# Modulation vectors on TensorE: groups of two row blocks in place of one

## The chip, the cores and the metric

One core of one Trainium2 chip. The metric is the device time of one execution in microseconds; the median of three runs of the kernel before is 2575.46 us (2573.92 to 2581.18).

## What is computed

A backbone of two layers over 256 latent and 256 context tokens, 1024 channels wide. Each layer makes six modulation vectors per stream from a conditioning vector, and uses them around its norms and residuals:

```python
mod  = jnp.split((sc @ p['w_mod'] + p['b_mod'])[:, None, :], 6, axis=-1)
modc = jnp.split(sc_ctx @ p['w_mod'] + p['b_mod'], 6, axis=-1)
h = modulate(rmsnorm(x, p['norm1_g']), mod[0], mod[1])
y, yc = token_mixer(h, hc, p, lambda_init, ctx_out)      # projection, 3 mixers, merge
x = x + mod[2] * y
h2 = modulate(rmsnorm(x, p['norm2_g']), mod[3], mod[4])
x = x + mod[5] * ec_moe(h2, p)                           # 16 experts, top-32 tokens each
```

The context stream goes through the same steps in the first layer. w_mod is 1024 x 6144 per layer, so one vector needs a 1024 x 1024 piece of it: eight row blocks of 128 rows, 512 KB each.

## The kernel before

Everything is computed with the channels on the partitions. A layer is a mixer (`run_blocks`: a list of projection blocks of 128 output channels, 24 matmuls each in three fp32r passes) and then a mixture of experts (`moe`, `body`), whose expert weights stream in through the SP queue. The first layer's mixer runs from about 60 to 930 us, its out-projection to about 990, its experts to about 1480; then the same for the second layer.

The order of all instructions is written out when the kernel is built. The blocks of `run_blocks` are the foreground. Between their matmuls `Background.pump` lets generator tasks (attention heads "diff", long convolutions "hy", the convolution's filters, modulation vectors) run one step each, up to the next `yield wait(...)`. A step may run when the planner's own clock has passed its due time, when a PSUM bank is free, and when its gate, if it has one, is open. The list of live tasks is walked in order, and at most four (WIDTH, first layer) are live in the first place. `until` and `drain` run steps early where the foreground would wait.

Modulation vectors of the first layer come three ways. Vectors 0 and 1 are made in `setup`. Vectors 2, 3 and 4 of layer 0 and 0 and 1 of layer 1 are the task "modN" (line 2020), vector 5 of layer 0 is the task "modA" (line 1584), both by `mod_run` (line 708). `mod_run` keeps `depth` row blocks in flight. For each block it issues four matmuls, one for each 256 of the 1024 columns, into four 32-column tiles of the array (the stationary operand `sc` is 32 columns wide); then it waits for a free "a4" buffer (the gate `room(a4=1)`), issues the next 512 KB load (`mod_load`), and waits for the oldest block in flight and a pause in the planner's time: 6000 ns for modN, 1300 ns for modA. After eight blocks `mod_out` copies the sum out, transposes it on PE and adds the bias; `mod_post` prepares the router (`router_prep`) after vector 4.

The a4 pool has 13 buffers of 512 KB. The projection's raw weights (`wraw`, loaded by `load_block` up to three blocks ahead), their two fp32r halves (`wh`, `wl`), key tiles of the attention and the modulation row blocks (`wm`) share it. `load_block` takes one only while more than one (SPARE) is free. At the start of the first layer's experts, expert weights use it too: `body` fills them, forces the rest of modA (`drain("modA")`, line 1945) and fills on. modN has to be done before the out-projection's `pre_out` (line 1562).

Of the kernel before, what the change touches and what calls it, by code (L numbers as in the profile page):

```python
# [21 lines left out]
KT = 8  # L22
# [249 lines left out]
def wait(*aps, delay=0.0, bank=1, gate=None):  # L272
    return aps, delay, bank, gate
# [135 lines left out]
class Kernel:  # L409
# [298 lines left out]
    def mod_run(self, vs, depth, pause, delay=3000.0):  # L708
        todo = [(l, v, k) for l, v in vs for k in range(KT)]
        raw = deque(self.mod_load(*todo.pop(0)) for _ in range(depth))  # L710
        yield wait(raw[0], delay=delay)
        for l, v in vs:
            acc = self.bank([128, 256], "m")
            for k in range(KT):
                w = raw.popleft()
                for c in range(4):
                    self.mm(acc[c * 32:(c + 1) * 32, :], self.sc[:, k, :], w[:, c * 256:(c + 1) * 256], k == 0, k == KT - 1, 4)
                w = None
                if todo:
                    yield wait(gate=self.room(a4=1))  # L720
                if todo:
                    raw.append(self.mod_load(*todo.pop(0)))
                yield wait(*list(raw)[:1], delay=pause)
            yield wait(acc, bank=0)
            yield from self.mod_out(l, v, acc)
            yield from self.mod_post(l, v)
# [668 lines left out]
    def mixer(self, l):  # L1395
        nc, A = self.nc, self.A
        full = l < L - 1
# [12 lines left out]
        def add(srcs, hl, n, evac, pre=None, drains=()):  # L1410
            bl.append(Block(srcs, hl, n, evac, pre, drains))

        def cols(w, c0, n=128):
            return [((slice(0, 128), slice(0, KT), slice(0, n)), w.rearrange("(k p) n -> p k n", p=128)[:, :, c0:c0 + n])]
# [161 lines left out]
        for j in range(KT):  # L1576
            def ev_o(p, j=j):
                for s in range(ns):
                    sl = slice(s * 256, s * 256 + 256)
                    self.stt(self.xT[:, j, sl], p[:, sl], self.modc[l][:, 2, j, s:s + 1], self.xT[:, j, sl], OP.mult, OP.add)  # L1580
                self.bg.add("post", lambda task, j=j: self.post(l, j, nq))
                if j == 4 and full:
                    vs = [(l, 5)]
                    self.bg.add("modA", lambda task: self.mod_run(vs, 2, 1300.0, 19000.0 if full else 11000.0))
            add(cols(A["w_out"][l], j * 128), lambda: self.mg, nt, ev_o, pre_out if j == 0 else None)
        return bl

# [429 lines left out]
    def run(self):  # L2017
        bl = self.mixer(0)
        self.setup(bl)
        self.bg.add("modN", lambda task: self.mod_run([(0, 2), (0, 3), (0, 4), (1, 0), (1, 1)], 1, 6000.0))  # L2020
        for l in range(L):
            if l:
                self.new_arena(3)
                self.lend(2)
                self.bg.add("filter", lambda task: self.transform(task), 2)
            fill, body = self.moe(l)
            self.fill = fill
            self.bg.layer = l
            self.run_blocks(bl)
            body()  # L2030
            if l < L - 1:
                bl = self.next
                for b in bl[EARLY:3]:
                    self.split_block(b)
                self.make_h(self.norm_next(), l + 1)
        self.final()
# [27 lines left out]
```

## Time and profile before

| | us |
|---|---|
| median of three runs | 2575.46 |
| lowest, highest | 2573.92, 2581.18 |
| the profiled execution | 2579.04 |
| its span, first to last instruction | 2577.3 |
| PE busy | 2240.2 |
| DVE busy | 1347.2 |
| ACT busy | 882.1 |
| POOL busy | 794.8 |

The mean granted TensorE clock of the profiled execution is 0.945 of full. PE is the engine of the matrix products, PEld its weight loads, DVE, ACT and POOL the vector, scalar and general engines, SP the queue that issues nearly all DMAs. The profile gives two records to each fp32 matmul. "Idle before" and "waited for" are worked out from semaphore events; a wait is put down to the event that came last.

### The profile page before, as it was taken

What the parts mean: (1) busy time and instruction counts of PE and PEld (TensorE: products, weight loads), DVE (VectorE), ACT (ScalarE), POOL (GpSimd) and SP (SyncE); (2) the same over time, 40 slices, a digit from 0 to 9 for tenths busy, and PEclk for the clock granted to TensorE, in tenths of its full rate; (3) what the DMA queues carried; (4) which work ended last, traced back from release to release, by engine and by line L of the source; (5) the groups of instructions that cost most, each with busy time, mean ns of one, the idle gap of its engine ahead of it and who ended that gap; (6) DMA issues with size and microseconds to landing.
All of it is one profiled execution on the core that took longest, in us unless ns stands there. A gap on an engine that the chain in (4) does not pass through costs nothing.

```text
span 2577.3 us, 38619 instructions
## 1 busy us (share of the span) xinstructions
PE 2240.2 (87%) x14970; PEld 1542.7 (60%) x14970; DVE 1347.2 (52%) x2907; ACT 882.1 (34%) x1933; POOL 794.8 (31%) x775
## 2 busy tenths in 40 slices
PE   6999998989999998989998899899888987656565
PEld 4777776767768775333333378878787864323223
DVE  4778778888672324223333178887887541101011
ACT  4445444555552332101111055556435441000001
POOL 2653433642334541000111055665544430000000
PEclk8999999999999999999999999999989989878787
DMA  9434233221213368899999963333665589999997
GB/s 304 123 122 126 89 109 106 58 66 50 66 58 91 95 252 316 331 428 417 398 400 399 398 185 97 104 95 84 177 190 164 130 317 423 422 424 423 424 423 278
DMA packets 327135, 590.32 MB, mean 229 GB/s; under 512 B 46076, under 2 KB 278184, under 8 KB 299304
## 3 DMA queue, kind: packets, MB, share of 16 engines
q1 hardware_dynamic: 326952, 587.85, 62.2%
q8 instruction: 119, 1.95, 0.3%
q14 instruction: 64, 0.52, 0.1%
HBM read 584.66 MB, written 3.15 MB: 228 GB/s over the span
## 4 chain that ended last, share of the span: by engine, by line
PE 47%; DMA 20%; DVE 20%; issue 4%; ACT 4%; POOL 3%; SPq 1%; DVEq 0%; POOLq 0%; ACTq 0%
PE p L458 44%; DMA mw<-in_moe_w_dram 19%; DVE arena L261 6%; DVE t L261 5%; PE p L469 3%; DVE wl L261 2%; DVE qp L261 2%; ACT arena L261 1%; DMA wm<-in_w_mod_dram 1%; POOL wl L261 1%; SPq L261 1%; POOL arena L261 1%; DVE ma L261 1%; DVE yc L261 1%; ACT wh L261 1%
## 5 line engine op out<-in xcount | busy, mean ns | idle before, releaser
L458 PE MATMUL p<-mw,xg 128*32 128x256 f32 (+1 forms) x3072 | 411.0, 508 | 115.3 <-DMA mw<-in_moe_w_dram 114.4
L458 PE MATMUL p<-hhi,wh 128*128 128x512 f32 (+1 forms) x1344 | 471.4, 363 | 10.1 <-DVE arena L261 7.7
L458 PE MATMUL p<-hlo,wh 128*128 128x512 f32 (+1 forms) x1344 | 458.9, 354 | 1.6 <-POOL hlo L261 0.8
L261 POOL TENSOR_TENSOR wl<-wraw,wh 128x512 fp32r<-128x512 f32 x232 | 342.5, 1478 | 374.8 <-ACT wh L261 251.8
L458 PEld LDWEIGHTS p<-mw,xg 128*32 128x32 f32 (+1 forms) x3072 | 133.7, 129 | 317.1 <-issue 200.0
L458 PE MATMUL p<-hhi,wl 128*128 128x512 f32 (+1 forms) x1344 | 312.9, 361 | 4.5 <-DVE wl L261 4.4
L458 PEld LDWEIGHTS p<-hhi,wh 128*128 128x128 f32 x1344 | 259.4, 193 | 48.5 <-issue 13.3
L458 PEld LDWEIGHTS p<-hlo,wh 128*128 128x128 f32 x1344 | 259.6, 193 | 31.4 <-POOL hlo L261 1.7
L458 PE MATMUL p<-mw,aT 128*32 128x256 f32 (+3 forms) x1760 | 200.4, 475 | 62.5 <-DMA mw<-in_moe_w_dram 58.2
L261 DVE TENSOR_TENSOR wl<-wraw,wh 128x512 fp32r<-128x512 f32 x231 | 217.0, 940 | 57.4 <-ACT wh L261 47.0
L261 ACT ACTIVATE wh<-wraw 128x1024 fp32r<-128x1024 f32 x232 | 241.4, 1053 | 9.0 <-DMA wraw<-in_w_in_dram 6.8
L458 PEld LDWEIGHTS p<-hhi,wl 128*128 128x128 f32 x1344 | 222.0, 194 | 37.0 <-DVE wl L261 5.2
L261 ACT ACTIVATE arena<-p 128x512 f32<-128x512 f32 (+1 forms) x212 | 106.4, 507 | 354.5 <-PE p L458 296.7
L458 PEld LDWEIGHTS p<-mw,aT 128*32 128x32 f32 (+1 forms) x1760 | 79.5, 134 | 172.3 <-issue 109.0
L261 DVE COPY yS<-p 32x512 f32<-32x512 f32 (+1 forms) x60 | 33.4, 556 | 272.9 <-ACT yS L261 272.9
L261 POOL TENSOR_TENSOR sq<-sq,sq 128x512 f32<-128x512 f32 (+1 forms) x6 | 6.3, 1055 | 505.6 <-ACT sq L261 498.8
L458 PE MATMUL p<-yb,wh 128*128 128x512 f32 (+1 forms) x768 | 153.6, 343 | 7.5 <-POOL yb L261 6.8
L261 ACT ACTIVATE arena<-p,t 128x512 f32<-128x512 f32 (+1 forms) x192 | 116.5, 613 | 84.7 <-DVE t L261 82.5
L458 PEld LDWEIGHTS p<-yb,wh 128*128 128x128 f32 x768 | 118.5, 190 | 26.8 <-POOL yb L261 11.6
L261 ACT ACTIVATE s<-p 128x512 f32<-128x512 f32 (+1 forms) x32 | 15.7, 491 | 337.1 <-PE p L458 336.9
L261 ACT ACTIVATE yS<-p 32x256 f32<-32x256 f32 (+2 forms) x84 | 35.3, 420 | 266.2 <-PE p L458 247.1
L469 PE MATMUL p<-cst,arena 128*128 128x128 f32 x608 | 101.0, 290 | 28.8 <-DVE arena L261 27.8
(243 smaller groups left out, 3451.4 us busy)
## 6 DMA issues: line engine op xcount, KB each, us to landing
mw<-in_moe_w_dram SPq DMA_DIRECT2D x171, 2048.0 KB
wraw<-in_w_in_dram SPq DMA_DIRECT2D x152, 512.0 KB
wm<-in_w_mod_dram SPq DMA_DIRECT2D x72, 512.0 KB
mw<-in_moe_w_dram SPq DMA_DIRECT2D x46, 512.0 KB
mw<-in_moe_w_dram SPq DMA_DIRECT2D x17, 1024.0 KB
wraw<-in_w_branch_dram SPq DMA_DIRECT2D x32, 512.0 KB
wm<-in_w_mod_dram SPq DMA_DIRECT2D x5, 2048.0 KB
wraw<-in_w_in_dram SPq DMA_DIRECT2D x32, 256.0 KB
```

Source lines behind the costliest of these rows:

```text
L261: return f(*args, **kw)
L458: self.nc.tensor.matmul(out, lhsT=lhsT, rhs=rhs, start=start, stop=stop, skip_group_check=tiles > 1)
L469: self.nc.tensor.transpose(out, in_, self.ident[:n, :n])
```

## The change

`mod_run` works on `depth` row blocks at a time: the matmuls of all of them, then a gate for `depth` a4 buffers, then `depth` loads, each still 512 KB, then a wait for all of them. modN goes from depth 1 with a pause of 6000 to depth 2 with 12000; modA keeps depth 2, and its pause goes from 1300 to 2600. The start delay of modA loses a branch that was never taken, since the task is only added where `full` holds.

```diff
     def mod_run(self, vs, depth, pause, delay=3000.0):
         todo = [(l, v, k) for l, v in vs for k in range(KT)]
         raw = deque(self.mod_load(*todo.pop(0)) for _ in range(depth))
-        yield wait(raw[0], delay=delay)
+        yield wait(*raw, delay=delay)
         for l, v in vs:
             acc = self.bank([128, 256], "m")
-            for k in range(KT):
-                w = raw.popleft()
-                for c in range(4):
-                    self.mm(acc[c * 32:(c + 1) * 32, :], self.sc[:, k, :], w[:, c * 256:(c + 1) * 256], k == 0, k == KT - 1, 4)
+            for k0 in range(0, KT, depth):
+                for k in range(k0, k0 + depth):
+                    w = raw.popleft()
+                    for c in range(4):
+                        self.mm(acc[c * 32:(c + 1) * 32, :], self.sc[:, k, :], w[:, c * 256:(c + 1) * 256], k == 0, k == KT - 1, 4)
                 w = None
                 if todo:
-                    yield wait(gate=self.room(a4=1))
-                if todo:
+                    yield wait(gate=self.room(a4=depth))
+                for _ in range(min(depth, len(todo))):
                     raw.append(self.mod_load(*todo.pop(0)))
-                yield wait(*list(raw)[:1], delay=pause)
+                yield wait(*raw, delay=pause)
...
-                    self.bg.add("modA", lambda task: self.mod_run(vs, 2, 1300.0, 19000.0 if full else 11000.0))
+                    self.bg.add("modA", lambda task: self.mod_run(vs, 2, 2600.0, 19000.0))
...
-        self.bg.add("modN", lambda task: self.mod_run([(0, 2), (0, 3), (0, 4), (1, 0), (1, 1)], 1, 6000.0))
+        self.bg.add("modN", lambda task: self.mod_run([(0, 2), (0, 3), (0, 4), (1, 0), (1, 1)], 2, 12000.0))
```

## Rows read from the trace of the kernel before

**Rows 1.** The page's table of engines: busy us, share of the span, instructions.

```profile
PE 2240.2 (87%) x14970; PEld 1542.7 (60%) x14970; DVE 1347.2 (52%) x2907; ACT 882.1 (34%) x1933; POOL 794.8 (31%) x775
```

**Rows 2.** Busy us and instructions by stage, granted clock (share of full), DMA share, GB/s.

```profile
60.00:460.00 400.00, 374.88 (x2110) 288.35 (x2109) 313.00 (x657) 184.15 (x396) 193.48 (x210) 0.98 0.37 113
460.00:930.00 470.00, 450.23 (x2409) 356.14 (x2408) 286.33 (x649) 218.41 (x486) 189.45 (x173) 1.00 0.27 76
1000.00:1480.00 480.00, 442.06 (x2273) 176.52 (x2273) 143.99 (x338) 63.70 (x146) 36.77 (x65) 0.99 0.96 391
```

**Rows 3.** Chain that ended last, by line: first of 60 to 460 us, then 1000 to 1480.

```profile
by line: PE p L458 43.8%; DVE arena L261 17.0%; issue 6.7%; DVE t L261 6.0%; PE p L469 3.8%; DVE qp L261 3.2%; ACT arena L261 2.7%; DVE wl L261 1.9%; DVE yc L261 1.8%; POOL arena L261 1.8%; ACT qp L261 1.3%; DVE yd L261 1.0%; DMA wraw<-in_w
by line: PE p L458 64.4%; DMA mw<-in_moe_w_dram 26.3%; PE p L469 2.3%; DVE yS L261 1.3%; ACT yS L261 1.2%; DVE arena L261 1.1%; issue 0.8%; POOL hx L261 0.6%; DVE xg L261 0.5%; DVE s L261 0.4%; DVE sr L261 0.3%; ACT hx L261 0.3%; POOL K L26
```

**Rows 4.** PE's timeline around one modulation group: start us, us, engine, line, operation, out<-in.

```profile
108.42 0.40 PE L458 MATMUL p<-hhi,wh 128*128 128x512 f32 x1
108.66 0.40 PE L458 MATMUL p<-hlo,wh 128*128 128x512 f32 x1
108.98 0.64 PE L458 MATMUL p<-wm,sc 128*32 128x256 f32 x8
109.56 0.50 PE L458 MATMUL p<-hhi,wh 128*128 128x512 f32 x1
109.89 0.40 PE L458 MATMUL p<-hlo,wh 128*128 128x512 f32 x1
```

**Rows 5.** PE's timeline at the end of layer 0's out-projection, modulation groups and top-k transposes.

```profile
985.77 0.64 PE L458 MATMUL p<-wm,sc 128*32 128x256 f32 x8
...
989.04 2.37 PE L458 MATMUL p<-wm,sc 128*32 128x256 f32 x40
...
994.25 0.64 PE L458 MATMUL p<-wm,sc 128*32 128x256 f32 x8
998.54 0.42 PE L469 MATMUL p<-cst,mk 32*128 32x32 f32 x2 [3.65 <-DVE mk L261]
```

**Rows 6.** Instructions of tile wm: engine, operation, count, duration ns min/median/max.

```profile
L458 PE MATMUL p<-wm,sc x576: 379/403/636, 22.6 to 1507.2; 128*32 128x256 f32 x192
```

**Rows 7.** First and last group on PE; second and last load on SP (timelines).

```profile
65.12 0.64 PE L458 MATMUL p<-wm,sc 128*32 128x256 f32 x8
448.72 0.64 PE L458 MATMUL p<-wm,sc 128*32 128x256 f32 x8
67.34 0.34 SPq L261 DMA_DIRECT2D wm<-in_w_mod_dram  x1
440.29 0.34 SPq L261 DMA_DIRECT2D wm<-in_w_mod_dram  x1
```

**Rows 8.** Tile wraw until 106 us, one split on ACT, one piece of the chain.

```profile
L261 SPq DMA_DIRECT2D wraw<-in_w_in_dram x13: 367/379/3665, 22.2 to 104.3; - x13
L261 ACT ACTIVATE wh<-wraw x9: 1042/1057/1067, 29.9 to 94.8; 128x1024 fp32r<-128x1024 f32 x9
134.23 1.05 ACT L261 ACTIVATE wh<-wraw 128x1024 fp32r<-128x1024 f32 x1
90.63 3.61 DMA wraw<-in_w_in_dram
```

**Rows 9.** SP's timeline of modA's loads and the expert weights behind them.

```profile
950.87 22.51 SPq L261 DMA_DIRECT2D wm<-in_w_mod_dram  x8
977.41 102.35 SPq L261 DMA_DIRECT2D mw<-in_moe_w_dram  x29
```

**Rows 10.** Busy us by stretch as in rows 2: two with low clock, one after modN.

```profile
300.00:340.00 40.00, 38.84 (x208) 30.61 (x207) 22.49 (x44) 17.45 (x36) 12.32 (x14) 0.93 0.32 93
420.00:460.00 40.00, 34.78 (x191) 27.27 (x190) 33.17 (x63) 13.21 (x28) 23.22 (x19) 0.91 0.31 97
460.00:540.00 80.00, 71.47 (x363) 57.91 (x362) 68.24 (x106) 47.67 (x101) 51.63 (x48) 1.00 0.23 59
```

**Rows 11.** PE's timeline just after router_prep.

```profile
301.53 0.63 PE L458 MATMUL p<-hlo,wh 128*128 128x512 f32 x1
```

## The prediction

> **What bounds the kernel now.** I read the page's engine table first, then the stages, then the chain, and last the timelines around the modulation matmuls. PE is busy 87% of the span and is the busiest engine [rows 1]. By stage: from 60 to 460 us, where all of modN's groups lie, PE is busy 374.88 of 400 us and the DMA engines have a share of 0.37, so loading has room there; from 1000 to 1480 the experts' weights fill the DMA engines (0.96) [rows 2]. A reader would now call the first stretch PE-bound. The chain of waits corrects this: of 60 to 460 us only 43.8% is matmul and 3.8% transposes, 47.6% together; most of the rest goes through DVE (attention, filter and convolution steps) [rows 3]. So a microsecond taken from PE in this stretch is worth about half a microsecond, unless the DVE steps move up with it. The experts' chain is 64.4% matmul and 26.3% weight DMA [rows 3]; nothing of the change lies in it but modA's end.
>
> **What one group costs.** In an undisturbed stream the projection matmuls start 0.24 us apart (108.42 to 108.66). The group of one row block starts 0.32 after the matmul before it, the next projection matmul 0.58 later, and the one after that 0.33 later [rows 4]. From 108.66 to 109.89 that is 1.23 us, where two pitches would take 0.48: one block put in alone costs 0.75 us. A block that follows another is cheaper: where modA's blocks run five in a row, 40 records take 2.37 us, against 0.64 for the 8 records of one, so (2.37 - 0.64) / 4 = 0.43 for each further block [rows 5]. The 0.32 between 0.75 and 0.43 is the price of going into the four-tile matmuls and out again, paid once a group. Two blocks cost 1.50 as two groups and 1.18 as one.
>
> The Trainium skill weighs in against the change here: TensorE: Matmul & The Clock Gate, Part 3, "The mechanism", states that weight loads overlap running matmuls only where the row group differs, and all of a group's tiles use the same 128 rows. By that the second block could not load under the first, would cost 0.75 like the first, and the sum below would be nothing. The run of 40 records contradicts it with 0.43, so I keep the row.
>
> **How many.** The 576 records of tile wm [rows 6] are two for each of 288 matmuls: 64 in setup, 160 in modN (5 vectors, 8 blocks, 4 columns), 32 in modA, 32 in the second layer's vector 2, which the change does not touch. modN's 40 groups of one become 20 of two. PE loses 20 x 0.32 = 6.4 us. The matmuls, their number and the sums stay. On the path it is 6.4 x 0.476 = 3.0 us; the bounds are 0 (every group lies in a stretch where DVE ends last) and 6.4 (DVE's steps move up with PE).
>
> **What moves.** The loads: 40 of 512 KB either way, on SP, now two behind one another. From the second load at 67.34 to the last at 440.29 the 38 steps are 9.81 us apart [rows 7], 6 of them the pause and 3.8 the rest (the step's turn, the gaps at a vector's end). If the rest stays per step, a pair takes 15.8 us and modN's last group comes at about 65 + 20 x 15.8 = 380 instead of 448.72 [rows 7]; an estimate, since the pause is in the planner's time. Its vectors are first used after 930 us, so neither an earlier nor a later end is on the path by itself. What changes with it is one of four task slots, free some 70 us sooner.
>
> The added wait for both transfers: nothing else is queued behind it, as only this task's next step waits, and PE's stream goes on with other work. A pair has 12 us of pause where one 512 KB transfer takes 3.61 from issue [rows 8]. I take nothing; the bound above is the second transfer's own 3.6 us at each of 20 pairs if SP held it back, which no wait of before suggests.
>
> The gate for two a4 buffers, and one more buffer held for most of the stretch: by 106 us 13 wraw loads are out and 9 blocks are split, so the load at 104.31 serves the fourth split from there, at 134.23, 29.9 us later [rows 8]. Less the 3.61 for landing, 26 us of cover remain; a buffer less takes one block from it, some 9 us (29.9 over the three blocks and a part that lie between). I take nothing for the projection. For the task itself a shut gate only postpones modN, which has 480 us of slack. Cover gone altogether would cost up to 3.6 us a block.
>
> modA keeps its depth; its waits go from one block to pairs. Its eight blocks sit where PE waits for the top-k chain on DVE (idle 3.65 us before 998.54) [rows 5], so fewer groups gain nothing. Its loads are issued 950.87 to 973.38, and the expert weights follow on SP at 977.41 [rows 9]. As long as all eight stay ahead of those, nothing moves. The dropped branch of the delay was never taken.
>
> **The sum.** 2579.04 (the profiled execution, 3.58 above the median) - 3.0 = 2576.0; against the median, 2575.46 - 3.0 = 2572.4. With the bounds 0 and 6.4 the forecast's own range is 2569.1 to 2575.5, and about 5 us wider on either side for the new order of background steps.
>
> **The rivals.** *Background better packed.* modN leaves its slot some 70 us sooner, and another attention or convolution task starts then. For it: PE idles 5.2 us in 420 to 460 and 8.5 us in 460 to 540 [rows 10], just where modN's end falls. Against it: the chain is on DVE half the time, and more tasks do not speed DVE up. If half of the 13.7 us of idling goes, the time is 2572.4 - 6.9 = 2565.5, and with all 6.4 us of the groups 2562.1; I take 2564.
>
> *modA's last pair falls behind the expert weights.* Place: SP at 977 to 1001 us. If the planner lets the third pair's step wait past the first fill, the last two loads queue behind up to 6 MB of expert weights (four single blocks of 512 KB and two chunks of 2 MB); at the 391 GB/s of that stage [rows 2] that is 16 us, and the forced end of modA stands on PE ahead of the first gather. At the chain's 66% PE (64.4% and transposes) the price is 11 us, so 2583. It decides when the fourth pair is loaded after the fill. Against it: seven of eight blocks are done by 991.41, before the top-k chain, and the eighth at 994.25 [rows 5]; pairs with the doubled pause should keep that rhythm.
>
> *A worse order.* The steps' places change, and with them which gaps open. Just after router_prep a projection matmul takes 0.63 us instead of 0.40 [rows 4, 11]; the granted clock falls to 0.93 over 300 to 340 and 0.91 over 420 to 460 [rows 10], which is 0.14 x 40 and 0.18 x 40 us at the lower level (1.2 of 2.4 GHz), half of it lost: 2.8 and 3.6 us. Three more such falls make +9.6 with the groups' gain kept, 2582.
>
> *It does not do what it says.* The gate keeps shutting or steps come late, and the gain goes into waits of the same size: 2575.5.
>
> **How the numbers follow.** 0.3% of the time, about what a measurement of this kernel tells from no change, is 7.7 us: faster is below 2567.7, slower above 2583.2. The forecast has 0.50 (0.44 within, 0.06 faster), better packing 0.29 (faster), modA 0.05 (slower), a worse order 0.10 (0.07 slower, 0.03 within), no effect 0.06 (within). Faster 0.35, within 0.53, slower 0.12. The range goes from 2560, under the packing case's 2562, to 2584, over the 2583 and 2582 of the slower cases; what lies outside is under 2 in 10.
>
> **What would show it.** modN's matmuls in 20 runs of 16 records of about 1.07 us; PE's busy time down by some 6 us; two wm loads in a row on SP; modN's last group at 370 to 400. The start of the out-projection and of the experts should both come 2 to 6 us sooner. If the mixer ends much sooner than that, it is packing, seen as less idling on PE between 380 and 540. If the mixer is sooner but the end is not, look at SP around modA. The prediction is wrong if the chain of 60 to 460 is as long in its DVE pieces with a changed PE, or if wraw loads come late and PE waits for wl.

## The result, and the profile after

The changed kernel takes 2598.93 us (median of 4 runs, 2597.23 to 2603.65) against 2577.01 for the kernel before on the same chip: a ratio of 1.0086, 95% interval 1.0071 to 1.0101. It is slower, and outside the forecast range. Its profiled execution takes 2599.19 us, with a span of 2597.4, 20.1 more than before.

The table of engines in the profile of the changed kernel [rows 1]:

```profile
PE 2238.9 (86%) x14970; PEld 1549.9 (60%) x14970; DVE 1338.6 (52%) x2907; ACT 880.9 (34%) x1933; POOL 795.9 (31%) x775
```

The work is the same: the same instructions. The time was lost in one place. The following table has the start of the first matmul of some projection blocks (24 matmuls each, counted through both layers; 116 and up are the second layer's), in us, read from the two traces:

```
block   before    after   difference
   3      62.0     62.8      +0.8
  23     240.6    231.0      -9.6
  43     439.0    423.7     -15.4
  51     511.4    504.1      -7.2
  52     520.3    563.8     +43.6
  63     630.9    657.1     +26.2
  67     659.7    686.4     +26.6
 115     979.0   1005.7     +26.6
 119    1523.2   1550.4     +27.2
 231    2098.5   2123.6     +25.1
```

The changed kernel is ahead by 15.4 us at block 43, then 51 us are lost between blocks 51 and 52 (the stand, in what follows), and 17 are given back by block 63. From there on it stays between 25 and 29 us behind. The work from the start of block 3 to that of block 67, before and then after (us; busy us and instructions of PE, PEld, DVE, ACT, POOL; granted clock, DMA share, GB/s):

```profile
62.00:659.70 597.70, 559.29 (x3165) 433.44 (x3165) 470.26 (x1024) 294.04 (x662) 273.63 (x293) 0.99 0.32 95
```

```profile
62.80:686.40 623.60, 567.61 (x3166) 451.78 (x3166) 463.52 (x1024) 293.36 (x662) 274.77 (x293) 0.95 0.31 91
```

Of the 25.9 us that this work takes longer, 17.6 are idling of PE (56.0 in place of 38.4), and 8.3 are PE being busy longer with the same instructions, at a granted clock of 0.95 in place of 0.99.

PE's timeline of the changed kernel around block 52 (start us, us, engine, line, operation, out<-in, count, idle before it and its releaser), cut to the matmuls that matter:

```profile
508.36 1.16 PE L458 MATMUL p<-arena,arena 128*128 128x128 f32 x8 [0.41 <-ACT arena L261]
...
511.57 1.64 PE L458 MATMUL p<-hhi,wl 128*128 128x512 f32 x6
...
520.30 1.09 PE L469 MATMUL p<-cst,arena 128*128 128x128 f32 x4 [3.43 <-DVE arena L261]
522.64 2.08 PE L458 MATMUL p<-arena,arena 128*128 128x128 f32 x8 [1.26 <-ACT arena L261]
...
537.34 1.49 PE L458 MATMUL p<-arena,svt 128*64 128x128 f32 x16
...
554.17 1.94 PE L469 MATMUL p<-cst,arena 128*128 128x128 f32 x8 [4.61 <-ACT yf L261]
...
561.80 0.88 PE L458 MATMUL p<-yf,ft 128*128 128x256 f32 x6
563.42 0.66 PE L469 MATMUL p<-cst,yt 128*128 128x128 f32 x4 [0.75 <-ACT yt L261]
563.83 0.48 PE L458 MATMUL p<-hhi,wh 128*128 128x512 f32 x1
```

Block 51's last matmuls start at 511.57, block 52's first at 563.83. In between no projection matmul runs, only attention (`kp,qp`, `svt`), transposes and, at its end, the inverse of a long convolution (`yf,ft`). Before, block 52 followed block 51 thus:

```profile
519.72 0.70 PE L458 MATMUL p<-hhi,wl 128*128 128x512 f32 x2
520.26 0.40 PE L458 MATMUL p<-hhi,wh 128*128 128x512 f32 x1
```

The same 48 us in both kernels, first before, then after (columns as above):

```profile
516.00:564.00 48.00, 41.86 (x238) 32.84 (x237) 41.54 (x88) 29.48 (x72) 23.27 (x24) 1.00 0.26 66
```

```profile
516.00:564.00 48.00, 30.99 (x170) 23.69 (x169) 38.11 (x118) 26.42 (x83) 9.31 (x14) 0.72 0.05 12
```

PE works 11 us less, at a granted clock of 0.72, and the loads nearly stop.

What block 52 waits for can be read from the convolution. The last `yf,ft` matmuls, a convolution's inverse, as the views of tile yf from 440 to 620 us show them, before and after (count, duration ns, first and last start):

```profile
L458 PE MATMUL p<-yf,ft x36: 278/283/387, 457.7 to 492.0; 128*128 128x256 f32 x36
```

```profile
L458 PE MATMUL p<-yf,ft x48: 278/283/583, 457.5 to 562.4; 128*128 128x256 f32 x48
```

Before, the last of these matmuls starts at 492.0, 28 us ahead of block 52. After, it starts at 562.4, and block 52 follows 1.4 us later. DVE's timeline of the changed kernel shows where that convolution stood:

```profile
486.17 6.83 DVE L261 TENSOR_TENSOR arena<-arena,K 128x512 f32<-128x512 f32 x4
...
548.23 0.76 DVE L261 TENSOR_TENSOR yc<-arena 128x256 f32<-128x256 f32 x2
```

The products with the filter K are done at 493.0; its next step on DVE, `yc`, starts at 548.23. In the kernel before, that step follows the last products by 3.2 us (473.9 to 477.00). In the program this step has a gate: `yield wait(a, bank=0, gate=None if j else self.room(a2=5))`, five free a2 buffers of nine, for `yf` and `yc`. The attention heads take a2 buffers one at a time (`qp` with a gate of one, `yd` and `kl` with a gate of three). Block 52 is the first gate block of the mixer (it computes the gate that a branch's output is multiplied with), and its `pre` begins with `drain("hy")`: it forces background steps, whosever are due, until no convolution is left.

The attention heads are not the only ones that take a2 buffers here. The projection itself takes two at block 48, for the value tiles `svt` of the attention with a window (line 1504 of the kernel before), and one at block 50 for its key tile (`sk`, line 1512). The two of `svt` stay taken: filled before the stand, they are first read in it, at 537.34.

```profile
L261 DVE COPY svt<-p x2: 677/680/684, 502.0 to 503.9; 128x512 f32<-128x512 f32 x2
```

In the order that the changed program writes out, the last convolution comes to its gate in block 50, with three of the nine buffers free: `svt` holds two and one attention head four (`yd`, `kl`, two `qp`). Without the two of `svt` five would be free. A second head starts there, and at block 52 none is left. In the order of the kernel before, the last convolution is past this gate in block 47, ahead of `svt`.

### The profile page after: what moved, and what is told of

Read it like the earlier page. It is cut to its first block, busy times and chain, and to the rows that moved or that the text cites. A ratio compares the mean times of both kernels' runs of the same rounds, so it can differ in the third digit from the quotient of the medians.

```text
span 2597.4 us, 38648 instructions
## 1 busy us (share of the span) xinstructions
PE 2238.9 (86%) x14970; PEld 1549.9 (60%) x14970; DVE 1338.6 (52%) x2907; ACT 880.9 (34%) x1933; POOL 795.9 (31%) x775
## 4 chain that ended last, share of the span: by engine, by line
PE 46%; DMA 22%; DVE 19%; issue 4%; POOL 4%; ACT 4%; SPq 0%; DVEq 0%; POOLq 0%; ACTq 0%
PE p L458 43%; DMA mw<-in_moe_w_dram 20%; DVE arena L261 6%; DVE t L261 5%; PE p L469 3%; DVE wl L261 2%; DVE qp L261 2%; ACT arena L261 1%; DMA wm<-in_w_mod_dram 1%; POOL wl L261 1%; POOL arena L261 1%; DVE yc L261 1%; DVE ma L261 1%; ACT wh L261 1%; POOL yb L261 0%
## 5 line engine op out<-in xcount | busy, mean ns | idle before, releaser
L458 PEld LDWEIGHTS p<-hhi,wh 128*128 128x128 f32 x1344 | 259.0, 193 | 45.7 <-issue 10.2
L458 PE MATMUL p<-mw,aT 128*32 128x256 f32 (+3 forms) x1760 | 194.7, 457 | 58.8 <-DMA mw<-in_moe_w_dram 56.5
```

The lines of the kernel that those rows point to most:

```text
L458: self.nc.tensor.matmul(out, lhsT=lhsT, rhs=rhs, start=start, stop=stop, skip_group_check=tiles > 1)
```

## The experiments

None of these kernels leaves out any of the work. The ratios are to the kernel before on the same chip, whose medians there lie between 2573.22 and 2575.89 us.

**Which half of the change.** First modN alone in pairs, modA through a copy of the old function (shown against the kernel before, the new `mod_run` left out here):

```diff
+    def mod_old(self, vs, depth, pause, delay=3000.0):      # mod_run of before
...
-                    self.bg.add("modA", lambda task: self.mod_run(vs, 2, 1300.0, ...))
+                    self.bg.add("modA", lambda task: self.mod_old(vs, 2, 1300.0, ...))
...
-        self.bg.add("modN", lambda task: self.mod_run([...], 1, 6000.0))
+        self.bg.add("modN", lambda task: self.mod_run([...], 2, 12000.0))
```

> Only modN works in pairs (pause 12000, gate for two buffers); modA is as before. Theory A (the loss arises in the first layer's mixer, where the last long-convolution task is forced to its end ahead of the first gate block): the loss of the changed kernel is kept, about 2597 to 2600 us, with the gap of some 47 us between the projection blocks 51 and 52. Rival B (modA in pairs puts its last loads behind the expert weights): the loss is gone, about 2573 to 2577.

Measured: 2599.32 us, 1.0096 (1.0079 to 1.0113), with block 55 41.6 us late; the order of PE's instructions is that of the changed kernel up to 1011 us. Then modA alone in pairs, modN as before (the changed `mod_run` with depth 1 and a pause of 6000 for modN; shown against the changed kernel):

```diff
-        self.bg.add("modN", lambda task: self.mod_run([...], 2, 12000.0))
+        self.bg.add("modN", lambda task: self.mod_run([...], 1, 6000.0))
```

> Only modA works in pairs with its pause of 2600; modN is one block at a time with 6000, as before. Theory A: as before, 2576 to 2580 us, modA's forced end being worth at most 2 us. Rival B: most of the 22 us lost, 2595 or more.

Measured: 2576.82 us, 1.0009 (0.9996 to 1.0022). The loss is all modN's.

**The buffer and the load, without the pairs.** The kernel before with two row blocks of modN in flight, matmuls and steps one by one:

```diff
-        self.bg.add("modN", lambda task: self.mod_run([...], 1, 6000.0))
+        self.bg.add("modN", lambda task: self.mod_run([...], 2, 6000.0))
```

> The kernel before, with modN keeping two row blocks in flight instead of one, but still working through them one at a time with a pause of 6000. PE's instructions stand in the very order of before; only modN's loads come one step earlier and one more a4 buffer is held. Theory A (the order of the steps is what costs): no difference, 2575 to 2580 us. Rival C (one more held buffer makes the raw weights late): a loss of 10 us or more, 2587 and above, seen as PE waiting for wl or the splits waiting for wraw.

Measured: 2577.24 us, 1.0010 (0.9999 to 1.0021). PE's instructions stand in the same order as before; a second a4 buffer held and each load one group earlier cost nothing that can be measured.

**The starved convolution.** The changed kernel, in which attention leaves a2 buffers alone while a convolution stands at its gate:

```diff
+        self.owes = 0
...
         for j, (sa, a) in enumerate(ys):
+            if j == 0:
+                self.owes += 1
             yield wait(a, bank=0, gate=None if j else self.room(a2=5))
+            if j == 0:
+                self.owes -= 1
...
-        yield wait(q.ap, k.ap, bank=0, gate=self.room(a4=1, a2=3))
+        yield wait(q.ap, k.ap, bank=0, gate=lambda: self.room(a4=1, a2=8 if self.owes else 3)())
...
-            yield wait(bank=0, gate=self.room(a2=1))
+            yield wait(bank=0, gate=lambda: self.room(a2=6 if self.owes else 1)())
```

> The changed kernel, pairs and all, with one addition: while a long-convolution task stands at its gate for five free a2 buffers, the attention heads may start no new row or key pair unless six (a row) or eight (a head) are free, so the convolution gets its five. Theory A (the convolution is starved of a2 buffers by the attention heads and then forced): the gap between blocks 51 and 52 goes back to some 5 us and the time to 2568 to 2576, the pairs' own gain of 3 to 6 us showing. Rival C (pairs, buffers or loads cost by themselves): it stays above 2590.

Measured: 2579.76 us, 1.0021 (1.0009 to 1.0032). The stand is gone: block 55 is 11.1 us ahead of the kernel before, block 63 12.4. Up to the stand this kernel runs in the changed kernel's order (DVE's first 758 instructions are the same, and PE's up to 493 us); then the convolution's `yc` follows its products by 1.6 us and not by 55:

```profile
483.75 6.85 DVE L261 TENSOR_TENSOR arena<-arena,K 128x512 f32<-128x512 f32 x4
...
492.21 2.92 DVE L261 TENSOR_TENSOR yc<-arena 128x256 f32<-128x256 f32 x2
```

So the a2 buffers were what the convolution lacked. But the expected 2568 to 2576 was missed, since the lead is lost between blocks 63 and 71: block 71 is 7.6 us behind. The attention held off comes after. From block 63 to block 67 PE has 271 records here and 165 before, and DVE's work from 640 to 660 us, before and then here, has more than doubled:

```profile
640.00:660.00 20.00, 20.00 (x102) 15.84 (x101) 6.81 (x16) 7.85 (x16) 8.98 (x7) 1.00 0.34 86
```

```profile
640.00:660.00 20.00, 20.00 (x130) 15.80 (x129) 15.25 (x43) 12.22 (x29) 5.56 (x5) 1.00 0.22 62
```

The same gate from its other side, one number in the changed kernel:

```diff
-            yield wait(a, bank=0, gate=None if j else self.room(a2=5))
+            yield wait(a, bank=0, gate=None if j else self.room(a2=4))
```

> The changed kernel whole, with one number altered: a long convolution starts its inverse once four a2 buffers are free in place of five; its pool of nine, the pairs and the attention heads' own gates stay. If the last convolution starves at this gate (my theory), it now gets its buffers before the first gate block, the stand of about 50 us between the projection blocks 52 and 55 is gone, and the time comes to 2572 to 2583. If the stand has another cause (the pairs' loads, the clock, the attention heads themselves), the gate is beside the point and the time stays near 2598.

Measured: 2576.82 us, 1.0007 (0.9995 to 1.0018). DVE's timeline and tile yf of this run:

```profile
479.14 2.38 DVE L261 TENSOR_TENSOR arena<-arena,K 128x512 f32<-128x512 f32 x2
...
484.11 2.83 DVE L261 TENSOR_TENSOR yc<-arena 128x256 f32<-128x256 f32 x2
```

```profile
L458 PE MATMUL p<-yf,ft x48: 275/283/563, 450.6 to 500.9; 128*128 128x256 f32 x48
```

Between products and `yc` lie 2.6 us in place of 55, and the last inverse starts its last matmul at 500.9, ahead of block 52 (the stand lies between blocks 51 and 52, not 52 and 55 as the expectation has it). This run is the weaker of the two: an earlier convolution is let through sooner, so the order differs from 273 us on, and the last convolution is past its gate before `svt` is taken. With three buffers free, as in the changed kernel, a gate of four would have been shut too. With the buffers given back or asked for less, the loss of 0.9% is gone both times.

In this order, without a stand, the pairs bring no gain. From block 3 to block 67 PE is busy 5.4 us less than in the kernel before and idles 5.0 us more:

```profile
61.80:659.00 597.20, 553.85 (x3165) 439.93 (x3165) 466.43 (x1024) 292.97 (x662) 274.63 (x293) 0.98 0.32 95
```

**What the 0.32 us a group are worth.** The kernel before with its order of instructions, in which the four matmuls of an even row block are issued with the odd block's:

```diff
+            kept = []
             for k in range(KT):
-                w = raw.popleft()
-                for c in range(4):
-                    self.mm(acc[c * 32:(c + 1) * 32, :], ...)
+                kept.append((k, raw.popleft()))
+                w = kept[-1][1]
+                for c in range(4):
+                    self.model.op("PE", ...)                  # the planner counts as before
+                if vs[0] == (l, 5) or k % 2 == 1:
+                    for kk, w in kept:
+                        for c in range(4):
+                            self.nc.tensor.matmul(acc[c * 32:(c + 1) * 32, :], ...)
+                    kept.clear()
```

> The kernel before with its order of steps left as it is: modN and modA still step one block at a time, but the four matmuls of every even block are left out at their own place and issued together with those of the odd block behind it. All other instructions of PE stand in the order of before, so only the going in and out of the four-tile matmuls is saved 20 times in modN. By the forecast's bounds: 0 to 6.4 us faster, 3.0 by the share of PE in the chain, so 2572 against 2575. By the page's rule that the second block cannot load under the first: no gain, or a loss, since the first block of a pair comes later.

Measured: 2581.74 us (12 runs), 1.0021 (1.0008 to 1.0034). The same work, from the start of block 3 to that of block 67, here (the kernel before is shown with the result):

```profile
61.30:662.50 601.20, 555.47 (x3165) 437.81 (x3165) 468.92 (x1024) 294.30 (x662) 273.29 (x293) 0.98 0.32 94
```

PE is busy 3.8 us less and idles 45.7 us in place of 38.4, 7.3 more. That is beyond what single executions differ by: in the runs with modA alone in pairs and with two blocks in flight, whose PE order is that of before, PE idles 38.4 and 37.7 us over the same blocks. What PE waited for from 60 to 460 us (us, times, longest), before and here:

```profile
PE p L469 <- DVE arena L261: 5.4, 4, 3.0
PE p L458 <- DVE arena L261: 4.0, 2, 3.0
PE p L458 <- DVE qp L261: 3.5, 6, 0.8
...
PE p L458 <- POOL arena L261: 1.0, 2, 0.8
```

```profile
PE p L469 <- DVE arena L261: 7.9, 6, 4.2
PE p L458 <- DVE qp L261: 5.3, 8, 0.9
PE p L458 <- POOL arena L261: 4.1, 3, 2.3
...
PE p L458 <- DVE arena L261: 3.5, 2, 2.6
```

The freed time has become waiting for DVE and POOL: these four rows grow from 13.9 to 20.8 us. Saved PE time was worth nothing in this stretch. The time lies outside the forecast's 0 to 6.4 us of gain. The other expectation, no gain or a loss, came true, but not for its reason that the second block cannot load under the first, since PE's busy time did fall.

**Is it the pairs, or one unlucky order?** The changed kernel with other pauses for modN:

```diff
-        ... self.mod_run([...], 2, 12000.0))
+        ... self.mod_run([...], 2, 13000.0))     # then 11000.0, then 16000.0
```

> The changed kernel with modN's pause at 13000 instead of 12000. In its order of instructions the last long convolution is done ahead of the first gate block without being forced. Theory A (only the forced convolution costs): 2568 to 2576 us, no gap between blocks 51 and 52. Rival D (working in pairs delays the other tasks whatever the pause): 2590 or more.

> The changed kernel with modN's pause at 11000 instead of 12000. In its order of instructions the last long convolution is again forced ahead of the first gate block. Theory A: the gap of some 47 us between blocks 51 and 52 is there and the time is 2595 to 2605 us. If the time is near 2575, a forced convolution is not what costs.

> The changed kernel with modN's pause at 16000. The last long convolution is not forced in its order. Theory A: 2568 to 2576 us. Rival D: 2590 or more. Together with the pause of 13000 it shows how far two orders without a forced convolution lie apart.

Measured: with 13000 2576.75 us, 1.0008 (0.9994 to 1.0022); with 11000 2593.31, 1.0068 (1.0045 to 1.0090), 17.0 us ahead at block 51 and 33.2 late at block 55; with 16000 2583.42, 1.0028 (1.0012 to 1.0044). With 13000 and 16000 there is no stand at block 52. So pairs can starve the convolution or not, by the pause alone. The expected ranges were missed: 13000 and 16000 lie 0.8 and 7.4 us above that of Theory A, and 11000 lies 1.7 us under its own. With 16000 the order costs 0.3% without any stand.

The kernel before with another pause:

```diff
-        ... self.mod_run([...], 1, 6000.0))
+        ... self.mod_run([...], 1, 7000.0))
```

> The kernel before, one row block at a time, with modN's pause of 6000 made 7000, so that the order of the background steps is another one and nothing else is altered. If a change of the order alone is worth up to half a per cent either way as long as the last convolution is not forced, the time lies between 2565 and 2585 with no stand at block 52. If any shift of modN's steps from the pause of before brings the convolution's stand, it comes to 2590 or more.

Measured: 2580.24 us, 1.0019 (1.0009 to 1.0029), no stand; 24.7 us ahead at block 31, 9.0 behind at block 67. An early lead is given back here too.

The orders written out by these programs agree on one point. In each without a stand, the last convolution is past its gate before block 48 takes the `svt` buffers; the one exception is the run that holds attention off. Where it comes later (pauses of 12000 and 11000), it stands.

**Five background tasks.** The changed kernel, and then the kernel before, with one more live task in the first layer:

```diff
-WIDTH = (4, 3)
+WIDTH = (5, 3)
```

> The changed kernel whole, with five background tasks live in the first layer in place of four, which leaves every buffer pool as it is. If too few slots had held the last convolution back until the attention heads had the a2 buffers, it starts sooner with a fifth slot, is done before the first gate block, and the time comes to 2570 to 2585. If what counts is the number of a2 buffers and not the slots, a fifth task takes more of them, the convolution waits as long, and the time stays at 2595 or above.

> The kernel before with five background tasks live in the first layer in place of four; the modulation vectors stay in groups of one row block. It is the other half of the run with pairs and five slots, which came to 0.9976 of the kernel before. If the fifth slot alone brings that (nothing ahead of the first gate block is forced then, and the background ends sooner), the time is 0.996 to 0.999 of the kernel before, about 2567 to 2572. If the pairs bring it, with the starvation out of the way, the time here is that of the kernel before or above, 1.000 to 1.004, about 2573 to 2584.

Measured: with pairs 2568.56 us, 0.9976 (0.9966 to 0.9986), faster than both kernels and 1.4 us under its expected range; without pairs 2580.76, 1.0021 (1.0004 to 1.0038). The work of blocks 3 to 67 with pairs and five tasks, then without pairs:

```profile
62.50:652.40 589.90, 557.24 (x3166) 437.80 (x3166) 460.15 (x1024) 293.66 (x662) 276.75 (x293) 0.98 0.32 96
```

```profile
62.70:664.50 601.80, 563.35 (x3165) 438.36 (x3165) 466.66 (x1024) 294.36 (x662) 273.65 (x293) 0.97 0.32 94
```

The faster one idles 32.7 us on PE against 38.4 before and in its twin, and PE is busy 6.1 us less than in its twin; its last convolution's inverse is at 465.7. Whether pairs are needed for that, or this order is merely the best of those tried, stays open: the orders without a stand give ratios of 0.9976 to 1.0028 with pairs, and 1.0019 and 1.0021 for the two of single blocks that differ from before.

## Why the prediction was wrong

**What was right.** The price of a group: modN's matmuls are 20 runs of 16 records, each like the last one here, at 1.07 us = 0.64 + 0.43 [rows 4 to 6].

```profile
434.83 1.07 PE L458 MATMUL p<-wm,sc 128*32 128x256 f32 x16
```

The second block of a pair did load under the first, as the 0.43 had said. The weight loads of this pair, all sixteen, are over at 435.42, when the matmuls of the first block, 0.64 us long, still run:

```profile
434.83 0.59 PEld L458 LDWEIGHTS p<-wm,sc 128*32 128x32 f32 x16 [0.36 <-issue]
```

The rule that the Trainium skill gives (TensorE: Matmul & The Clock Gate, Part 3, "The mechanism") speaks against it; the 1.07 decides. Of the 6.4 us of PE, 3.8 were seen with the order kept, at a granted clock of 0.98 against 0.99. The wait for both transfers is free: from 55 to 460 us no wait of PE for a load of wm shows, and the one wait on tile wm is 0.4 us, of PE's weight loads. The held a4 buffer is free (the run with two blocks in flight), and so is modA, whose eight loads on SP stay ahead of the bulk of the expert weights exactly as in [rows 9]:

```profile
977.50 22.51 SPq L261 DMA_DIRECT2D wm<-in_w_mod_dram  x8
1004.04 2.14 SPq L261 DMA_DIRECT2D mw<-in_moe_w_dram  x3
```

**The step that failed first: "about 5 us wider on either side for the new order of background steps".** The measured loss is 21.9 us. I followed the a4 buffers, which the change names ("the gate for two a4 buffers"), and no others. A step that moves modN can move the convolutions and attention heads behind it, and these meet in the a2 pool: five at once for one, one at a time for the other, and two more for `svt` in block 48. The list of rivals had "a worse order" at 0.10, but priced as three falls of the granted clock, 9.6 us, and not as a forced task. Here the clock did fall (0.72 in the 48 us), but after PE had begun to idle; it is part of the price and not its start. The cost was a stand of 51 us. Of it 17 came back, because the forced steps needed no later place (from block 52 to block 63 PE has 483 records in place of 620), and 7 were covered by the lead at block 51. The number that would have given it room lay in the trace of before: 28 us from the last `yf,ft` at 492.0 to block 52 at 520.26. After the change the last convolution's forward matmuls (`uh,ft`) end 17 us later, 477.3 in place of 460.3, and block 51 comes 7 us sooner: 4 us of the 28 remain, even before a buffer is short. Shown by the runs: the stand is the convolution's, for want of a2 buffers. Read from the written order alone: who holds them. Not shown: why the pairs' double steps bring the last convolution to its gate so late, since with other pauses they do not.

**The term that failed next: "6.4 x 0.476 = 3.0 us".** A share of the chain was taken as the worth of each microsecond of PE. The merge in place gave a loss of 0.1 to 0.3% where that sum said a gain of 0.1%. The bound of zero was the nearer one. The run with the gate of four says the same: 5.4 us less of busy PE, 5.0 us more of idling. Why it is slightly below zero is not settled; the waits above show where, not why.

**The estimate of modN's end, 380 us.** It was 434.83. The sum counted 20 steps, where 20 pairs have 19 between the first and the last (365 us by its own step). From the first pair at 65.9 the 19 steps to it are 19.4 us apart, twice the single step's 9.81 [rows 7]: the 3.8 us beside the pause came twice a pair and not once, so the slot was free 14 us sooner, not 70.

**"Background better packed", 0.29.** The lead exists, 15.4 us at block 43, but it lies between blocks 3 and 43, not where modN ends, and of the orders that differ from before one alone is more than a microsecond ahead at block 71, the pairs with five tasks. A lead ahead of a gate block is an order's loan: from block 3 to block 51 PE has 2293 records in place of 2344, and the background steps are still to be done.

## What to carry over

Where background steps share pools, list for each pool who asks for several buffers at once and who takes them singly, the foreground too, and read from the trace how far ahead of the next forced drain the former ends; that margin, here 28 us, is what a reordering may use up. A share of the chain does not price time saved on an engine: idling beside it may grow by as much, so keep the order and change the one thing, and compare busy and idle time of the same work. With two kernels in which the order differs, compare the starts of the same blocks before anything else: one table showed that the loss arose between two of 232.

## Not expected of the hardware

The stand made PE's own work slower as well: eight 128x128 matmuls took 1.16 us at 508.36 and 2.08 at 522.64, after idle stretches of 3.43 and 1.26 us, and the granted clock of 540 to 560 us was 0.58. PE's idling comes first: it is busy 0.77 of 4 us in the slice from 516 us, at a granted clock of 0.92, and the next slice has 0.50 (columns as above):

```profile
512.00:516.00 4.00, 3.23 (x20) 2.52 (x18) 3.84 (x10) 2.67 (x5) 0.61 (x1) 1.00 0.00 0
516.00:520.00 4.00, 0.77 (x5) 0.37 (x3) 3.86 (x5) 1.50 (x5) 3.78 (x5) 0.92 0.00 0
520.00:524.00 4.00, 2.44 (x10) 2.07 (x11) 2.59 (x10) 3.68 (x11) 1.88 (x2) 0.50 0.02 4
```

```profile
540.00:560.00 20.00, 11.45 (x53) 8.38 (x54) 16.15 (x53) 8.88 (x26) 2.46 (x3) 0.58 0.00 1
```

So the forced steps that block 52 waited for ran, in good part, at the lower level of 1.2 GHz.
